# Longer waits between the bundles of the block inverse and ahead of the chain's first factors, in a hybrid decoder step on one core

## The chip, the cores and the metric

The kernel runs on 1 core of a Trainium2 chip. The metric is device time in microseconds of one launch, as the median of several runs; lower is better.

## What is computed

One step of a decoder layer: 2048 prompt tokens and 64 sample tokens (8 sequences of 8) go through two parallel head groups (sliding-window attention with sinks, and RWKV-7 with a matrix state), an output projection and a ConvFFN, each between RMS norms. Cut to what matters here:

```python
def step(S, inp):                        # RWKV-7, one token after the other
    r_t, w_t, k_t, v_t, kk_t, a_t = inp
    sa = einsum('bhij,bhj->bhi', S, kk_t)
    S = S * w_t - sa * (kk_t * a_t) + v_t * k_t
    return S, einsum('bhij,bhj->bhi', S, r_t)

proj = rms_norm(x) @ w_in                # q, k, v and the RWKV features
mix  = concat([attention(q, k, v), rwkv7(features)]) @ w_out
x    = x + rms_norm(mix)
x    = x + rms_norm(conv_ffn(rms_norm(x)))
```

All is in float32, and the outputs are both activations and the new caches and states.

## The kernel before

**Dense work.** The 2112 columns are cut into five groups of 448, 448, 448, 384 and 384. Each group has a projection `P[g]` (20 tasks of 24 matmuls), an output projection `O[g]` (8 tasks) and an FFN `F[2g]`, `F[2g+1]` (66 tasks). Every product is made of three matmuls of rounded halves (high by high, high by low, low by high), so that a task is 24 matmuls of 448 or 384 columns, named `gm` or `pf` in the trace; there are 470 tasks and 11,280 such matmuls. For each task ScalarE makes the high half of the weights (`wh`) and VectorE the low half (`wl`), two tasks ahead. A projection also spawns side streams (`pair`, `rest`, `norms`: matmuls `pw`, `pa`, `pd`, `pb`) that make the RWKV factors `ar` and `bk` and store them to memory as `abd`.

**Recurrent work.** The 32 chunks of 64 tokens are worked off in nine units of 3 or 4 chunks; a unit also holds one or two blocks of attention. `Mixer.unit` runs, for a unit, `scores` (matmuls `sc_e`, `sc_o` give each chunk's tile `G`), then `invert`, then `chain`, `groupnorm` and `finish`.

- `invert` (line 1011) inverts the triangular 32 by 32 blocks of `G`. It takes them through memory (`dgr`) into one tile `gb`, in which all blocks of a unit lie side by side, runs 31 steps of two VectorE instructions each (lines 1045 and 1046, on `tmp` and `tt`), in bundles of four, copies the result on ScalarE (line 1049), stores it twice (`dxr`, `dtr`), and loads it back into `G` (line 1059) and into the tiles `zt` (line 1088; two buffers). Then each chunk takes two groups of eight small matmuls (`pz`) with a ScalarE copy behind each.
- `chain` (line 1134) goes through the chunks in order, since each needs the state `S` that the one before left: transposes `vt` and `bkt` of the loaded values and factors (`ab<-abd`), matmuls `pc`, a ScalarE copy, `pu`, a ScalarE copy, `pS`, and two VectorE instructions that make the next `S` (lines 1175 and 1176).
- `groupnorm` and `finish` normalise on VectorE, transpose (`pt`), multiply by the gate (`pg`) and store to `od` (`od<-fin`), which `O[g]` loads (`r<-od`). `O[0]` needs units 0 and 1.

**The order.** The program is written as generators. `Flow` keeps a clock of its own, `Clock.t`, that adds up nominal matmul times in nanoseconds. A stream that yields a number N may go on once half of N has gone by on that clock (line 239 of `Flow.step`); between two dense matmul triples `Flow.tick` takes one step of a side stream and one of the unit in work. Where a stage needs something that isn't done, `Flow.force` runs the other streams with no dense work between them. A unit starts when the one before it has ended. The tile framework's scheduler then orders each engine's queue by this order and by its own view of what is ready. Each engine takes its queue strictly in order, and all transfers are issued by SyncE's queue.

`Flow.step` holds the line that turns a wait into planner's time:

```python
s.at = self.clock.t + (0.0 if callable(w) else 0.5 * (self.LAG if w is None else w))
```

The dense stages stand in this order:

```python
order = [P[0], P[1], P[2], O[0], P[3], F[0], O[1], F[1], P[4], F[2], O[2], ...]
```

Of the kernel before, what the change touches and what calls it, by code (L numbers as in the profile page):

```python
# [967 lines left out]
class Mixer:  # L968
# [43 lines left out]
    def invert(self, Gs):  # L1012

        nc, sp, v, te = self.nc, self.sp, self.nc.vector, self.te
        n = len(Gs)
        nb = n * 16
        dg = self.dp.tile([64, 1024], F32, tag="dg", name="dgr")

        def blocks(G, d, c):

            for b in range(2):
                for e in range(2):
                    q, r = slice(64 * e + 32 * b, 64 * e + 32 * b + 32), 16 * c + 8 * b + 4 * e
                    yield G[q, e::2, q], d[r:r + 4, :].rearrange("h (s t) -> s h t", t=32)

        for c, G in enumerate(Gs):
            for x, y in blocks(G, dg, c):
                nc.sync.dma_start(out=y, in_=x)
        yield 3000
        gb = self.b4([128, 32, 32], "gb", "ab")  # L1030
        nc.sync.dma_start(out=gb[:nb], in_=dg[:nb, :].rearrange("q (s t) -> q s t", t=32))
        tt = self.b4([128, 32, 32], "tt", "ab")

        tmp = sp.tile([128, 256], F32, tag="ivt", name="tmp", bufs=1)
        nc.gpsimd.memset(tt[:nb], 0.0)
        nc.gpsimd.memset(tt[:nb].rearrange("q s t -> q (s t)")[:, 0:1024:33], 1.0)
        yield 5000
        for j in range(31):
            if j and j % 4 == 0:
                yield 1500  # L1040
            m, w = 31 - j, j + 1
            col = gb[:nb, j, w:].unsqueeze(2).to_broadcast([nb, m, w])
            row = tt[:nb, j, 0:w].unsqueeze(1).to_broadcast([nb, m, w])
            tm = tmp[:nb, 0:m * w].rearrange("q (m w) -> q m w", w=w)
            v.tensor_tensor(out=tm, in0=col, in1=row, op=ALU.mult)  # L1045
            v.tensor_tensor(out=tt[:nb, w:, 0:w], in0=tt[:nb, w:, 0:w], in1=tm, op=ALU.subtract)  # L1046
        yield 1500
        xx = gb
        nc.scalar.copy(out=xx[:nb], in_=tt[:nb].rearrange("q s t -> q t s"))
        yield 1500  # L1050
        dx = self.dp.tile([64, 1024], F32, tag="dx", name="dxr")
        nc.sync.dma_start(out=dx[:nb, :], in_=xx[:nb].rearrange("q s t -> q (s t)"))
        dt = self.dp.tile([64, 1024], F32, tag="dt", name="dtr")
        nc.sync.dma_start(out=dt[:nb, :], in_=tt[:nb].rearrange("q s t -> q (s t)"))
        yield 3000
        zts = []
        for c, G in enumerate(Gs):
            for x, y in blocks(G, dx, c):
                nc.sync.dma_start(out=x, in_=y)
            if c < 2:  # L1060
                zts.append(self.zt(dt, c))
        yield 5000
        for c, G in enumerate(Gs):
            if c + 2 < n:
                zts.append(self.zt(dt, c + 2))
            zt = zts[c]

            q = [(slice(64 * e, 64 * e + 32), slice(64 * e + 32, 64 * e + 64)) for e in range(2)]
            hd = [slice(32 * p, 32 * p + 32) for p in range(4)]
            pz = self.ps("pz")  # L1070
            for h in range(NH):
                x, y = q[h % 2]
                te.matmul(pz[y, hd[h // 2]], G[x, h, y], zt[x, hd[h // 2]], start=True, stop=True)
            for x, y in q:
                nc.scalar.copy(out=zt[y], in_=pz[y, 0:128])
            yield 2500
            pz = self.ps("pz")
            for h in range(NH):
                x, y = q[h % 2]
                te.matmul(pz[x, hd[h // 2]], zt[y, hd[h // 2]], G[y, h, y], start=True, stop=True)  # L1080
            for e, (x, y) in enumerate(q):
                nc.scalar.activation(out=G[x, e::2, y], in_=pz[x, 0:128].rearrange("p (h t) -> p h t", t=32), func=AF.Copy, scale=-1.0)
            yield 1500
# [50 lines left out]
    def chain(self, c0, n, Gs, ys):  # L1134

        nc, v, te, sh = self.nc, self.nc.vector, self.te, self.sh
        uvs, nxt = {}, self.factors(c0)

        def values(c):
            t, w = CH * (c0 + c), CH * min(2, n - c)  # L1140
            V = self.t2("vl", tag="vl", bufs=1).rearrange("p (q t) -> p q t", t=128)
            nc.sync.dma_start(out=V[:, :, :w], in_=sh.v[:, :, t:t + w].rearrange("q p t -> p q t"))
            return V

        V = values(0)
        yield 5000
        for c in range(n):
            if c % 2 == 0:
                m = min(2, n - c)
                pv = self.ps("vt")  # L1150
                for p in range(4):
                    te.transpose(pv[:CH * m, 128 * p:128 * p + 128], V[:, p, :CH * m], sh.ident)
                for i in range(m):
                    uvs[c + i] = self.t2("uv", tag="uv", bufs=2)
                    self.values(uvs[c + i], pv[64 * i:64 * i + 64])
                yield 1500
            (ars, bks), uv, G = nxt, uvs[c], Gs[c]
            bkt = self.bk_tok(bks, "bkt")
            yield 1500
            if c + 1 < n:  # L1160
                nxt = self.factors(c0 + c + 1)
                if c % 2:
                    V = values(c + 1)
            S, Sn = sh.S[self.si], sh.S[1 - self.si]
            self.si = 1 - self.si
            pc = [self.ps("pc", "o") for _ in range(2)]
            for p in range(4):
                for e, a in enumerate(HH):
                    te.matmul(pc[e][:, 64 * p:64 * p + 64], ars[p][a], S[a, p, :], half=True, start=p == 0, stop=False)
            yield from self.solve(G, uv, pc)  # L1170
            pS = self.ps("pS")[:, 0:256]
            for p in range(4):
                for e, a in enumerate(HH):
                    te.matmul(pS[a, 64 * p:64 * p + 64], heads(bkt, e)[:, p], heads(uv, e)[:, p], half=True, start=True, stop=True)
            v.tensor_tensor(out=Sn, in0=pS.rearrange("q (p d) -> q p d", d=64), in1=S, op=ALU.add)
            v.tensor_tensor(out=Sn, in0=Sn, in1=sh.EC[:, c0 + c, :].unsqueeze(2).to_broadcast([128, 4, 64]), op=ALU.mult)
            yield 500
            if c % 2 == 0:
                ys.append(self.t2("y", tag="y", bufs=2))
            self.outputs(ys[-1][HH[c % 2]], G, uv, pc)  # L1180
            yield 2000
# [282 lines left out]
def heads(t, e):  # L1464

    return t.rearrange("s (p e d) -> s e p d", e=2, d=64)[:, e]
# [207 lines left out]
```

## Time and profile before

| | |
|---|---|
| runs | 2900.69, 2896.43, 2889.96 us; median 2896.43 |
| profiled execution | 2903.55 us, of which the span 2901.8 us |
| TensorE busy (matmuls, ends modelled) | 2769.6 us, 95% of the span |
| VectorE, ScalarE, GpSimd busy | 1961.2, 1411.5, 265.7 us |
| mean granted TensorE clock | 0.969 of full speed |
| DMA | 446.60 MB, 154 GB/s in the mean |

The page lists, for one execution, the busy time of each engine, the span in 40 slices, the chain of work that ended last, and the costliest groups of instructions. The views asked of the trace are: who waited for whom, the timeline of one engine in a window, and the busy time of each engine in a window with the granted clock. A matmul's duration in the timeline is longer than the distance to the next one, since matmuls are pipelined: the distance between two dense matmuls of 448 columns in the timeline is 0.20 us.

### The profile page before, as it was taken

The numbers are of one execution on the slowest core, as the hardware profiler recorded it, in microseconds if no ns is written. First come the engines' busy times: TensorE is split into PE (matmuls) and PEld (weight loads), VectorE is DVE, ScalarE is ACT, GpSimd is POOL, SyncE is SP. The second block draws the span as 40 slices with busy tenths as digits, with TensorE's granted clock in tenths as the row PEclk, the third lists the DMA queues.
The fourth block names the chain that finished last, engine by engine and source line by source line (L and its number), as shares of the span: only waits on it lengthen the run. The fifth ranks groups of instructions, "written<-read, shape, count | busy, mean of one in ns | idle before, by whom it ended". The sixth has DMA issues, their size and how long they took to land.

```text
span 2901.8 us, 46432 instructions
## 1 busy us (share of the span) xinstructions
PE 2769.6 (95%) x17003; PEld 2403.4 (83%) x17003; DVE 1961.2 (68%) x3892; ACT 1411.5 (49%) x2621; POOL 265.7 (9%) x521
## 2 busy tenths in 40 slices
PE   8997999899999999989899999999999999999997
PEld 6775776678778888868688888888899999999997
DVE  6884796759665775599566675796645765566556
ACT  6554555555545545445554455555333444344432
POOL 0010011001101010011000010001001001011110
PEclk9997999989989999989899999999999999999998
DMA  6674545656644343565644434674433654345433
GB/s 197 199 207 130 177 139 174 189 176 186 182 129 128 124 133 119 160 210 163 179 133 131 131 113 138 218 230 123 125 109 110 195 175 127 128 143 167 129 126 104
DMA packets 312740, 446.60 MB, mean 154 GB/s; under 512 B 120648, under 2 KB 241160, under 8 KB 312496
## 3 DMA queue, kind: packets, MB, share of 16 engines
q1 hardware_dynamic: 312080, 443.48, 50.2%
q8 instruction: 134, 2.20, 0.3%
q14 instruction: 94, 0.77, 0.1%
q10 hardware_dynamic: 432, 0.16, 0.0%
HBM read 362.19 MB, written 76.97 MB: 151 GB/s over the span
## 4 chain that ended last, share of the span: by engine, by line
PE 52%; DVE 4%; DMA 2%; ACT 1%; issue 1%; SPq 0%; DVEq 0%; ACTq 0%
PE gm L185 32%; PE pf L185 14%; PE pc L185 1%; DVE wl L355 1%; PE ms L185 1%; ACT wh L354 0%; DMA r<-x2d 0%; PE po L185 0%; DMA w<-in_w 0%; PE sc L185 0%; PE sc_e L185 0%; PE pz L185 0%; PE ppt L189 0%; PE spc L185 0%; DMA r<-xnd 0%
## 5 line engine op out<-in xcount | busy, mean ns | idle before, releaser
L185 PE MATMUL gm<-xhi,wh 128*128 128x448 f32 (+3 forms) x2880 | 1045.9, 366 | 32.4 <-ACT xhi L354 11.1
L185 PE MATMUL gm<-xlo,wh 128*128 128x448 f32 (+4 forms) x2880 | 1035.9, 360 | 9.7 <-DVE xlo L355 9.6
L185 PE MATMUL gm<-xhi,wl 128*128 128x448 f32 (+4 forms) x2880 | 1032.6, 359 | 0.0
L354 ACT CAST wh<-w 128x1024 fp32r<-128x1024 f32 (+1 forms) x470 | 490.3, 1044 | 758.8 <-PE gm L185 408.5
L355 DVE TENSOR_TENSOR wl<-w,wh 128x1024 fp32r<-128x1024 f32 (+1 forms) x470 | 570.2, 1214 | 406.5 <-ACT wh L354 393.5
L185 PEld LDWEIGHTS gm<-xhi,wh 128*128 128x128 f32 (+2 forms) x2880 | 542.5, 189 | 100.0 <-issue 24.3
L185 PEld LDWEIGHTS gm<-xlo,wh 128*128 128x128 f32 (+2 forms) x2880 | 543.8, 189 | 58.5 <-DVE xlo L355 16.7
L185 PEld LDWEIGHTS gm<-xhi,wl 128*128 128x128 f32 (+2 forms) x2880 | 543.3, 189 | 40.2 <-issue 8.6
L185 PE MATMUL pf<-hh,wh 128*128 128x448 f32 (+1 forms) x880 | 319.5, 363 | 4.4 <-DVE c L895 2.7
L185 PE MATMUL pf<-hl,wh 128*128 128x448 f32 (+1 forms) x880 | 316.3, 359 | 0.0
L185 PE MATMUL pf<-hh,wl 128*128 128x448 f32 (+1 forms) x880 | 316.0, 359 | 0.0
L885 POOL COPY zcar<-zz 128x2 f32<-128x2 f32 x110 | 87.7, 797 | 1443.4 <-ACT zz L874 1443.4
L912 DVE TENSOR_TENSOR acc<-acc,pf 128x448 f32<-128x448 f32 (+1 forms) x200 | 117.9, 592 | 102.3 <-PE pf L185 101.6
L185 PEld LDWEIGHTS pf<-hh,wh 128*128 128x128 f32 x880 | 167.3, 190 | 21.0 <-issue 6.1
L185 PEld LDWEIGHTS pf<-hl,wh 128*128 128x128 f32 x880 | 167.5, 190 | 11.0 <-issue 2.8
L185 PEld LDWEIGHTS pf<-hh,wl 128*128 128x128 f32 x880 | 167.1, 190 | 10.6 <-issue 2.0
L881 DVE SCALAR_TENSOR_TENSOR c<-zz,c_cw,c 128x448 f32<-128x448 f32 (+2 forms) x220 | 140.9, 640 | 16.1 <-ACT c L875 13.3
L895 DVE TENSOR_TENSOR c<-c,gm 128x448 f32<-128x448 f32 (+1 forms) x110 | 65.1, 592 | 88.2 <-PE gm L185 78.8
L888 ACT ACTIVATE c<-c 128x448 f32<-128x448 f32 (+1 forms) x110 | 61.4, 558 | 129.3 <-DVE c L881 95.9
L1045 DVE TENSOR_TENSOR tmp<-gb,tt 64x31 f32<-64x31 f32 (+37 forms) x310 | 102.4, 330 | 7.8 <-DMA gb<-dgr 3.5
L1046 DVE TENSOR_TENSOR tt<-tt,tmp 64x31 f32<-64x31 f32 (+37 forms) x310 | 102.7, 331 | 4.4
L680 POOL COPY carry<-h 128x1 f32<-128x1 f32 (+1 forms) x70 | 45.4, 649 | 622.5 <-ACT h L678 622.3
(271 smaller groups left out, 3190.9 us busy)
## 6 DMA issues: line engine op xcount, KB each, us to landing
w<-in_w SPq DMA_DIRECT2D x220, 512.0 KB
w<-in_w2q SPq DMA_DIRECT2D x100, 512.0 KB
w<-in_w_all SPq DMA_DIRECT2D x90, 512.0 KB
ab<-abd SPq DMA_DIRECT2D x66, 512.0 KB
w<-in_w_out SPq DMA_DIRECT2D x40, 512.0 KB
r<-in_xT SPq DMA_DIRECT2D x40, 224.0 KB
r<-in_xT SPq DMA_DIRECT2D x32, 192.0 KB
r<-od SPq DMA_DIRECT2D x24, 224.0 KB
```

The costliest lines, as they stand in the source:

```text
L185: return self.te.matmul(out, lhsT, rhs, **kw)
L354: self.nc.scalar.copy(out=hi, in_=src)
L355: self.nc.vector.tensor_tensor(out=lo, in0=src, in1=hi.bitcast(F32), op=ALU.subtract)
L680: nc.gpsimd.tensor_copy(out=s.next[:m, i, :].unsqueeze(2), in_=hs[:, :, s.nl:])
L881: v.scalar_tensor_tensor(out=c[:, :npr], in0=z[:, j:j + npr], scalar=cw(j), in1=c[:, :npr], op0=ALU.mult, op1=ALU.add)
L885: nc.gpsimd.tensor_copy(out=sh.zcar[:, f, :], in_=z[:, npr:npr + 2])
L888: nc.scalar.activation(out=c, in_=c, func=AF.Silu)
L895: v.tensor_tensor(out=c, in0=c, in1=ps, op=ALU.mult)
L912: v.tensor_tensor(out=accs[c], in0=accs[c], in1=ps, op=ALU.add)
L1045: v.tensor_tensor(out=tm, in0=col, in1=row, op=ALU.mult)
L1046: v.tensor_tensor(out=tt[:nb, w:, 0:w], in0=tt[:nb, w:, 0:w], in1=tm, op=ALU.subtract)
```

## The change

Six numbers that streams yield are larger; no instruction is added or removed.

```diff
@@ invert
         nc.gpsimd.memset(tt[:nb].rearrange("q s t -> q (s t)")[:, 0:1024:33], 1.0)
-        yield 5000
+        yield 9000
         for j in range(31):
             if j and j % 4 == 0:
-                yield 1500
+                yield 6000
...
                 zts.append(self.zt(dt, c))
-        yield 5000
+        yield 14000
         for c, G in enumerate(Gs):
...
                 nc.scalar.copy(out=zt[y], in_=pz[y, 0:128])
-            yield 2500
+            yield 4000
             pz = self.ps("pz")
@@ chain
         V = values(0)
-        yield 5000
+        yield 9000
         for c in range(n):
```

Half of each number is planner's time: the step between two bundles of the inverse goes from 0.75 to 3.0 us of `Clock.t`, the wait for `zt` from 2.5 to 7.0, the one between the two `pz` groups from 1.25 to 2.0, the first factors' from 2.5 to 4.5. Counted along TensorE's dense matmuls, the changed program differs in these places.

TensorE's queue at the end of `P[1]`, where unit 0's inverse comes back (`pz`) and its chain begins (`vt`, `bkt`, `pc`, `pu`). Before:

```order
L185 MATMUL gm<-xhi,wl 128x448
L185 MATMUL pz<-zt,G 32x32
L189 MATMUL ppt<-c_ident,s 128x128 x2
L185 MATMUL pz<-zt,G 32x32 x7
L189 MATMUL ppt<-c_ident,s 128x128 x2
L185 MATMUL pz<-G,zt 32x32 x8
L189 MATMUL ppt<-c_ident,s 128x128 x4
L185 MATMUL po<-pT,va 64x512
L185 MATMUL pz<-zt,G 32x32 x8
```

And with the change:

```order
L185 MATMUL gm<-xhi,wl 128x448
L185 MATMUL pz<-G,zt 32x32
L185 MATMUL pz<-zt,G 32x32
L185 MATMUL pz<-G,zt 32x32 x7
L185 MATMUL pb<-b_2779,c_blockones 128x448
L185 MATMUL pz<-zt,G 32x32 x7
L185 MATMUL pw<-ls,lw_149 128x448
L185 MATMUL pz<-G,zt 32x32 x8
L185 MATMUL pz<-zt,G 32x32 x8
L185 MATMUL pz<-G,zt 32x32 x8
L185 MATMUL pz<-zt,G 32x32 x8
L185 MATMUL pz<-G,zt 32x32 x8
```

The first `pz` stood behind dense matmul 864 and stands behind 954 now, of the 960 of `P[0]` and `P[1]`; the attention's `ppt` and `po` are no longer among them, and the run of matmuls without a dense one, 100 long at 864, is 126 long at 960. The last step of the inverse moves from 864 to 927, counted by the dense matmuls ahead of it in the program.

TensorE's queue where unit 1's inverse comes back. Before, this is in the last fifth of `P[2]`, whose last dense matmul is 1439:

```order
L185 MATMUL gm<-xhi,wh 128x448
L185 MATMUL pz<-zt,G 32x32 x7
L185 MATMUL gm<-xlo,wh 128x448
L185 MATMUL gm<-xhi,wl 128x448
L185 MATMUL po<-pT,va 64x512
L185 MATMUL pz<-G,zt 32x32 x8
L185 MATMUL pz<-zt,G 32x32 x8
L185 MATMUL pz<-G,zt 32x32 x8
```

With the change:

```order
L185 MATMUL gm<-xhi,wl 128x448
L185 MATMUL pa<-ls,lw_153 128x448
L185 MATMUL pd<-d_160,sel_159 128x448
L185 MATMUL pb<-b_4644,c_blockones 128x448
L185 MATMUL pz<-zt,G 32x32 x8
L185 MATMUL pz<-G,zt 32x32 x8
L185 MATMUL pz<-zt,G 32x32 x8
L185 MATMUL pz<-G,zt 32x32 x8
L185 MATMUL pz<-zt,G 32x32 x8
L185 MATMUL pz<-G,zt 32x32 x8
L189 MATMUL vt<-c_ident,vl 128x128 x4
L189 MATMUL bkt<-c_ident,ab 128x128 x4
```

The `gm` ahead of it is the last of `P[2]`. The `pz` of unit 1 moved from 1331 to 1344 to behind 1440, and with them the whole chain, `groupnorm` and `finish` of the unit; 167 small matmuls follow each other there. The last step of the inverse moves from 1300 to 1435. Behind them stand 36 dense matmuls of `O[0]` that read the attention's half of `od`, and then the first that read unit 1's.

TensorE's queue in `P[3]`, at the start of unit 2's chain. Before:

```order
L185 MATMUL pz<-zt,G 32x32 x8
L185 MATMUL pz<-G,zt 32x32 x8
L189 MATMUL vt<-c_ident,vl 128x128 x4
L185 MATMUL pc<-S_117,ab 128x64
L189 MATMUL bkt<-c_ident,ab 128x128 x4
L185 MATMUL pc<-S_117,ab 128x64 x7
L185 MATMUL pc<-uv,G 64x64 x8
L185 MATMUL pu<-rhs,G 64x64 x8
L185 MATMUL pS<-uv,bkt 64x64
```

With the change:

```order
L185 MATMUL pz<-zt,G 32x32 x8
L185 MATMUL pz<-G,zt 32x32 x8
L185 MATMUL pz<-zt,G 32x32 x8
L185 MATMUL pz<-G,zt 32x32 x8
L189 MATMUL vt<-c_ident,vl 128x128 x4
L185 MATMUL gm<-xhi,wh 96x384
L185 MATMUL gm<-xlo,wh 96x384
L185 MATMUL gm<-xhi,wl 96x384
L185 MATMUL gm<-xhi,wh 96x384
```

Before, 125 matmuls without a dense one follow each other here, behind dense matmul 1728; now the longest such run is 36, at 1752, and 23 dense ones stand between `vt` and `bkt`.

## Rows read from the trace of the kernel before

**Rows 1.** The page's busy times, and the view of the core's span and clock.

```profile
PE 2769.6 (95%) x17003; PEld 2403.4 (83%) x17003; DVE 1961.2 (68%) x3892; ACT 1411.5 (49%) x2621; POOL 265.7 (9%) x521
...
core 0: 2901.8 us, clock 0.969
```

**Rows 2.** Who TensorE waited for: us in total, times, longest us.

```profile
PE pz L185 <- DMA zt<-dtr: 12.3, 7, 8.2
...
PE pb L185 <- DVE b L745: 8.0, 5, 2.5
...
PE pz L185 <- ACT zt L1075: 4.1, 7, 0.9
...
PE bkt L189 <- DMA ab<-abd: 3.6, 1, 3.6
```

**Rows 3.** Windows: length, busy (count) of PE, PEld, DVE, ACT, POOL, clock, DMA.

```profile
197.00:241.00 44.00, 40.60 (x180) 33.10 (x180) 41.37 (x110) 23.32 (x61) 2.71 (x8) 0.96 0.44 134
241.00:320.00 79.00, 61.98 (x594) 45.67 (x592) 32.26 (x63) 37.59 (x84) 2.99 (x10) 0.81 0.59 157
249.00:281.00 32.00, 23.44 (x217) 14.46 (x217) 9.29 (x14) 13.55 (x35) 2.04 (x4) 0.57 0.58 156
380.00:427.00 47.00, 45.22 (x216) 37.93 (x215) 46.43 (x119) 22.10 (x45) 10.09 (x11) 1.00 0.48 143
427.00:501.00 74.00, 71.54 (x581) 53.09 (x580) 46.07 (x97) 40.66 (x83) 8.82 (x13) 0.93 0.53 155
571.00:620.00 49.00, 43.88 (x377) 33.51 (x377) 28.26 (x69) 24.87 (x55) 1.69 (x4) 0.81 0.52 144
```

**Rows 4.** Timeline, unit 0's inverse and chain start: start us, us, engine, line, [idle before <-releaser].

```profile
242.78 0.51 SPq L1052 DMA_DIRECT2D dxr<-gb  x1
...
240.81 1.94 ACT L1049 COPY gb<-tt 64x1024 f32<-64x1024 f32 x1 [5.35 <-DVE tt L1046]
...
249.42 0.28 PE L185 MATMUL pz<-zt,G 32*32 32x32 f32 x2 [8.21 <-DMA zt<-dtr]
...
262.19 1.11 PE L189 MATMUL vt<-c_ident,vl 128*128 128x128 f32 x4
265.17 1.86 PE L185 MATMUL pb<-b,c_blockones 128*128 128x448 f32 x2 [1.85 <-DVE b L745]
...
272.11 1.09 PE L189 MATMUL bkt<-c_ident,ab 128*128 128x128 f32 x4 [3.63 <-DMA ab<-abd]
```

**Rows 5.** TensorE's timeline, one chunk of unit 0's chain at full clock.

```profile
283.74 1.11 PE L185 MATMUL pc<-S,ab 64*128 64x64 f32 x16
284.78 0.68 PE L185 MATMUL pc<-uv,G 64*64 64x64 f32 x16
...
286.20 0.78 PE L185 MATMUL pu<-rhs,G 64*64 64x64 f32 x16
...
288.81 0.47 PE L185 MATMUL gm<-xhi,wh 128*128 128x448 f32 x1
289.12 0.36 PE L185 MATMUL gm<-xlo,wh 128*128 128x448 f32 x1
289.32 0.36 PE L185 MATMUL gm<-xhi,wl 128*128 128x448 f32 x1
```

**Rows 6.** Timelines of three engines, unit 1's groupnorm and finish, and the start of `O[0]`.

```profile
474.07 0.68 DVE L1188 TENSOR_REDUCE st<-y 64x8 f32<-64x512 f32 x1
...
486.71 0.68 DVE L1199 TENSOR_TENSOR y<-y,rsg 64x512 f32<-64x512 f32 x1
...
491.49 0.38 SPq L358 DMA_DIRECT2D od<-fin  x1
...
496.08 0.37 SPq L358 DMA_DIRECT2D od<-fin  x1
...
487.70 0.74 PE L189 MATMUL pt<-c_ident,y 64*128 64x64 f32 x3
...
504.44 0.47 PE L185 MATMUL gm<-xlo,wh 128*128 128x448 f32 x1 [2.78 <-DVE xlo L355]
```

## The prediction

> **What bounds the kernel now.** I first read the busy times: TensorE is busy 95% of the span, at a mean clock of 0.969 [rows 1]. So no term can be large: what can be won is TensorE's idle time and the time in which its clock is granted at half, that is, at 1.2 instead of 2.4 GHz. The table of waits then says whom TensorE stood idle for. The inverse and the first factors have 12.3 us behind the transfer of `zt`, 4.1 behind ScalarE's copy into it and 3.6 behind the load of `ab`; side streams have others, such as 8.0 at `pb` behind VectorE [rows 2]. That is 20 us by name. But an idle stretch also costs clock, so I read the windows next, and in each one the loss as idle time plus busy time times what the clock lacks of 1 [rows 3]. In the 79 us from 241 (unit 0's inverse comes back and its chain runs) TensorE idles 79.0 - 62.0 = 17.0 us, and 62.0 x 0.19 = 11.8 go with the clock: 29 us, the dearest stretch that the change touches. In 571 to 620 (unit 2's) it is 5.1 + 43.9 x 0.19 = 13.4, in 427 to 501 (unit 1's chain) 2.5 + 71.5 x 0.07 = 7.5.
>
> Why unit 0 comes back so late is in the same view: from 197 to 241, while its inverse is computed, VectorE is busy 41.4 of 44 us, and from 380 to 427 (unit 1's) 46.4 of 47 [rows 3]. VectorE, not the planner's 0.75 us, paces the inverse. Its last step ends just before ScalarE's copy at 240.81; TensorE has run into `pz` by then and waits until 249.42 [rows 4].
>
> **Part one: the wait for `zt` and `ab` at the end of `P[1]`.** In the program before, the first `pz` of unit 0 stood right behind the last step of the inverse (both at dense matmul 864). Now 27 dense matmuls lie between (927 and 954). One takes 0.20 us (289.12 to 289.32 [rows 5]), so they cover 5.4 of the 8.6 us from 240.81 to 249.42 [rows 4]; about 3 of the 8.2 remain, a gain of 5. The 3.6 at `bkt` and the 1.9 at `pb` [rows 4] go, since the factors are fetched 4.5 planner's us before they are used and the side streams' groups now stand apart in the queue: 5.5. The remaining idle of the window (17.0 - 8.2 - 3.6 - 1.9 = 3.3) stays, and so does half of the clock: from 249 to 281 TensorE was busy 23.4 us at 0.57 [rows 3], which lost 10.1, and the run of small matmuls there is 126 long now, no shorter than before; I take 5. With 3 more for the stretch up to 241 (3.4 idle and 40.6 x 0.04 of clock), where the inverse no longer crowds VectorE, this is **-19 us**. Bounds: -5, if only the `zt` wait shrinks, and -29, the whole loss of the window.
>
> **Part two: unit 2 in `P[3]`.** The run of 125 small matmuls becomes short runs with dense ones between; nothing new is waited for. Of the 13.4 us, half of the idle and three quarters of the clock's part go: 2.6 + 6.3, **-9 us** (0 to -13).
>
> **Part three: the other units.** There remain 12.3 - 8.2 = 4.1 us behind `zt` and 4.1 behind ScalarE's copy [rows 2], against planner's waits that grow from 2.5 to 7.0 and from 1.25 to 2.0 us. I take all 8 as gone: **-8 us** (0 to -15, the latter with as much in clock).
>
> **Part four: what is now late, `O[0]`.** Unit 1 starts when unit 0 has ended and now ends later itself; `O[0]` needs it. Before, the two just met: the last store to `od` is issued at 496.08, and the first dense matmuls of `O[0]` wait only 2.8 us, at 504.44 [rows 6]. Now all of `P[2]`'s dense matmuls stand ahead of the first `pz` of unit 1, and the last step of the inverse is only five of them earlier. From there to the first matmul on unit 1's rows, nothing of `P[2]` is left to cover:
>
> - inverse to first `pz`: 8.6 us, as for unit 0 [rows 4];
> - three chunks of `pz`: four took 12.8 (249.42 to 262.19 [rows 4]), with six matmul groups of the attention between; taken 6 (at most 9.6);
> - `vt` and the copies behind it: 3, twice the way from `pc` to `pu` (284.78 to 286.20 [rows 5]);
> - three chunks: 283.74 to 288.81 is 5.1 [rows 5], with the two VectorE instructions for the new state some 6 each: 18;
> - `groupnorm`: 13.3 us from 474.07 to 487.39 [rows 6], shared with other VectorE work; taken 7;
> - `finish`: 487.70 to 496.08, 8.4 us [rows 6];
> - store, load and split: 242.78 to 249.42 is 6.6 for a store and the loads behind it [rows 4]; taken 7.
>
> That is 58; the first half of the rows is stored 4.6 us earlier (491.49 against 496.08 [rows 6]), so 53. Of these, 36 dense matmuls of `O[0]` cover 7, and about 18 are TensorE's own work on this chain, which it had to do anyway (three times some 4.3, of which 1.11, 0.68 and 0.78 stand in [rows 5], and 5 for the rest). Idle: 53 - 1 - 7 - 18 = 27; at the clock of unit 0's bare run (0.57), the 18 cost 8 more: 35. What it replaces: the 7.5 of unit 1's chain in `P[2]`, the 2.8 at `O[0]`, and some 3 of the crowded window from 380, since VectorE's 31 steps are spread over a longer piece of `P[2]`. Net **+22 us**. Bounds: +5 (a chain at the pace of its own instructions, idle 12) and +40 (`pz` and `groupnorm` at their upper figures, all at half clock).
>
> **The sum.** -19 - 9 - 8 + 22 = -14 us on the profiled execution's 2903.55 (span 2901.8 and 1.75 around it), that is 2889. That run lies 7.1 above the median of the runs, 2896.43, for which I forecast **2882**.
>
> The Trainium skill ("TensorE: Matmul & The Clock Gate", section "What's actually happening") puts the cost of the clock's ramp at under 1% of a typical kernel's span and advises against fitting it. The trace does not agree: a mean clock of 0.969 is 3.1% of the span, 90 us [rows 1].
>
> **Rivals.**
>
> *No change.* VectorE paces the inverse, whatever the planner's clock says, and the chain between `P[2]` and `O[0]` runs no faster than it did at 241 to 320, where four chunks, from the inverse's end to the end of their chain, filled the window's 79 us. Without the 96 dense matmuls between (20 us) that is 59, for three chunks 44, against 36 in my first four rows: 8 more, and with 3 more at the clock the sum is -3: 2893. For it: VectorE's 94 to 99% [rows 3]. Against it: 79 us contain the waits at `ab` and `pb`.
>
> *Slower.* The price is set by the length of runs without a dense matmul. Before, there were three such runs of 100, 67 and 125, which lost 29, 7.5 and 13.4; now there are two, 126 and 167 long. If both cost what the dearest did, 0.29 us for each small matmul, it is 84 against 50: +34, with the -8 of the other units +26: 2922. It decides when each of the two runs ends in a transfer, as the run at 241 did, and the one before `O[0]` ends in three (`zt`, `ab`, `od`). Against it: 427 to 501 held 581 matmuls and lost little, because dense ones stood between.
>
> *The clock costs nothing.* If the half clock falls only where TensorE waits anyway, the clock's terms drop out: part one gives 14, part two 3, part three 8, and part four costs 27 - 2.5 - 2.8 - 3 = 19: -6, 2890. This is what the page's rule above comes to. The window 249 to 281, busy 23.4 us of 32 at 0.57 [rows 3], speaks against it.
>
> **How the numbers follow.** My forecast's case, a gain of 5 to 45 us, has 0.50; no change 0.24; slower 0.20; the clock for nothing 0.06. A measurement of this kernel can tell about 0.5% (14 us) from no change, so the forecast's own time stands at that border: within its case I give a gain over 0.5% four fifths, because part four is counted piece by piece with little overlap: 0.40, and 0.05 from the others. Slower by over 0.5%: four fifths of the slower rival and a little of the no-change case: 0.19. The range goes from 2849 (the first three parts at their lower bounds, part four at +10) to 2924 (the slower rival).
>
> **What would show it.** Right: no wait at `bkt` behind `ab`; the waits of `pz` for `zt` under 6 us in total outside the stretch before `O[0]`; a new idle time of 20 to 35 us on TensorE just before `O[0]`, in pieces behind `zt`, ScalarE, VectorE and `od`, at a clock well under 1; unit 2's stretch at a clock over 0.95; the same count of instructions. Wrong: `O[0]` starting as soon as `P[2]` ends, which would make part four a gain; VectorE as full as before while TensorE waits at `pz` as long as before; or new stalls in `P[4]`, where unit 6's inverse now falls among the projection's pairs, for which I have no term.

## The result, and the profile after

| | before | changed |
|---|---|---|
| runs beside each other | 2896.44 us (2886.02 to 2900.69, 8 runs) | 2909.64 us (2903.79 to 2918.09, 8 runs) |
| ratio, 95% interval | | 1.0052 [1.0034, 1.0070] |
| profiled execution | 2903.55, span 2901.8 | 2906.23, span 2904.5 |

The changed kernel is 13 us slower, where the prediction had it 14 us faster; the interval reaches to both sides of the 0.5% that it took as the border of "no change". The profiled executions lie 7 above the median of before and 3 below that of the changed kernel, so the two traces differ by 3 us only. For that reason a second trace of the kernel before is used below (label before_again, 2881.90 us). One correction to the text ahead: the diff enlarges five numbers, not six.

The page's busy times of the changed kernel, and its span and clock, against [rows 1]:

```profile
PE 2770.7 (95%) x17003; PEld 2401.8 (83%) x17003; DVE 1962.9 (68%) x3892; ACT 1410.6 (49%) x2623; POOL 267.3 (9%) x521
...
core 0: 2904.5 us, clock 0.969
```

The sums are the same to a thousandth, but for GpSimd's (0.6% more); ScalarE counts two more instructions, both loads of its function tables. Whom TensorE waited for in the changed kernel (us in total, times, longest), against [rows 2]:

```profile
PE gm L185 <- ACT h L678: 13.1, 5, 5.1
PE rb_ps L185 <- DVE nr L51: 8.0, 1, 8.0
PE pb L185 <- DVE b L745: 7.9, 3, 4.9
...
PE ms L185 <- DVE dg L787: 7.1, 3, 3.8
...
PE pz L185 <- ACT zt L1075: 3.2, 6, 0.7
...
PE pz L185 <- DMA zt<-dtr: 2.0, 5, 0.7
```

The waits that the change aimed at are gone: 2.0 us behind `zt` in place of 12.3, none at `bkt` behind `ab`. In their place stand waits of the projection's pairs and of the norms: 13.1 at `h`, 8.0 at `nr`, 7.1 at `dg` (at `b` it is 7.9, as before). Two of these in the kernel before:

```profile
PE ms L185 <- DVE dg L787: 5.2, 3, 3.1
...
PE gm L185 <- ACT h L678: 4.1, 2, 2.5
```

Where the time went is read best along the dense work, which is the same in both kernels. I cut the span at the first matmul of tasks 30, 50, 80, 140 and 300 (task 40 begins `P[2]`, 60 `O[0]`, 68 `P[3]`, 162 `P[4]`, 182 `F[2]`), and take `P[4]` by itself as the fifth line. Windows of the kernel before, with the columns of [rows 3]:

```profile
201.20:402.30 201.10, 176.84 (x1132) 133.09 (x1131) 141.85 (x326) 101.17 (x227) 13.68 (x38) 0.91 0.55 157
402.30:691.10 288.80, 266.46 (x1871) 208.82 (x1870) 211.10 (x497) 155.26 (x342) 25.33 (x42) 0.92 0.59 176
691.10:1100.70 409.60, 403.47 (x2608) 338.56 (x2607) 282.54 (x613) 210.00 (x397) 45.49 (x58) 0.97 0.47 141
1100.70:2131.50 1030.80, 992.55 (x6404) 846.63 (x6403) 712.70 (x1469) 513.21 (x961) 83.46 (x166) 0.98 0.50 154
1256.50:1380.70 124.20, 116.61 (x646) 98.20 (x646) 112.42 (x252) 69.16 (x155) 25.14 (x68) 0.99 0.63 188
```

The same five of the changed kernel:

```profile
199.80:363.00 163.20, 157.06 (x1075) 123.99 (x1074) 127.71 (x283) 95.15 (x215) 21.16 (x36) 0.95 0.60 177
363.00:662.50 299.50, 265.59 (x1851) 208.36 (x1849) 211.93 (x503) 155.81 (x340) 30.44 (x44) 0.90 0.58 171
662.50:1074.50 412.00, 402.20 (x2654) 333.67 (x2653) 286.21 (x606) 204.72 (x389) 30.09 (x58) 0.99 0.47 140
1074.50:2134.20 1059.70, 1014.92 (x6436) 860.38 (x6435) 724.44 (x1513) 523.43 (x984) 87.89 (x166) 0.97 0.50 152
1239.90:1394.40 154.50, 138.99 (x822) 110.89 (x822) 115.17 (x271) 76.32 (x174) 28.68 (x68) 0.93 0.55 162
```

And the second trace of the kernel before, in the first four stretches:

```profile
200.40:398.20 197.80, 175.74 (x1131) 131.88 (x1131) 141.77 (x326) 101.09 (x227) 16.20 (x38) 0.91 0.56 160
398.20:679.60 281.40, 260.19 (x1871) 204.54 (x1871) 211.02 (x497) 154.83 (x341) 25.85 (x42) 0.95 0.61 180
679.60:1080.30 400.70, 395.17 (x2608) 331.19 (x2607) 282.36 (x613) 209.39 (x397) 44.46 (x58) 1.00 0.48 145
1080.30:2111.90 1031.60, 993.66 (x6404) 848.23 (x6403) 712.88 (x1469) 513.29 (x962) 81.51 (x166) 0.98 0.50 154
```

The reader should take the first number behind each window. Against the mean of the two traces of before (201.1 and 197.8, 288.8 and 281.4, 409.6 and 400.7, 1030.8 and 1031.6), the changed kernel gains 36 us in tasks 30 to 49, loses 14 in 50 to 79, 7 in 80 to 139 and 28 in 140 to 299: together 13, which is the difference of the medians. (Small matmuls count where they stand: 57 fewer stand in tasks 30 to 49 of the changed kernel, so that some 5 us of its gain there, an estimate from the pace of their forms, are work moved over the cut.) Up to task 139 the change is a gain of 15; the loss is behind that, where the prediction had a small gain. The fifth line names the place: `P[4]` takes 154.5 us in place of 124.2. There 176 more matmuls stand in it, most of them unit 6's, so part of the length is work that stood elsewhere before; but TensorE also idles 15.5 us in place of 7.6, and the clock is granted at 0.93 in place of 0.99.

The local windows of the changed kernel, in the order unit 0's inverse, unit 0's `pz` and first chunk, unit 1's inverse, the stretch ahead of `O[0]`, unit 2's chain:

```profile
196.00:251.00 55.00, 55.00 (x256) 45.13 (x257) 51.94 (x127) 33.66 (x80) 13.01 (x16) 1.00 0.65 191
...
258.00:285.00 27.00, 22.36 (x280) 16.84 (x280) 9.51 (x16) 13.53 (x38) 0.31 (x2) 0.68 0.52 147
...
383.00:436.00 53.00, 48.87 (x226) 38.49 (x227) 50.31 (x127) 25.40 (x52) 17.67 (x15) 1.00 0.57 163
436.00:500.00 64.00, 47.78 (x449) 36.82 (x448) 29.18 (x71) 27.13 (x62) 0.20 (x1) 0.73 0.58 165
...
575.00:650.00 75.00, 65.67 (x636) 52.69 (x635) 45.02 (x82) 42.12 (x95) 6.81 (x16) 0.86 0.63 198
```

In the first, VectorE is as full as before (51.9 of 55 us) and TensorE does not wait at all, at full clock. In the fourth, 16.2 us are idle and 47.8 x 0.27 = 12.9 go with the clock: 29 where the chain of unit 1 lost 7.5 before. TensorE's timeline of that stretch:

```profile
445.46 1.83 PE L185 MATMUL pb<-b,c_blockones 128*128 128x448 f32 x2 [4.88 <-DVE b L745]
...
453.11 1.11 PE L189 MATMUL vt<-c_ident,vl 128*128 128x128 f32 x4
...
486.70 1.07 PE L189 MATMUL pt<-c_ident,y 64*128 64x64 f32 x3 [2.64 <-DVE y L1199]
488.77 1.47 PE L189 MATMUL pt<-c_ident,y 128*128 128x128 f32 x4 [1.01 <-ACT fin L1219]
...
499.46 1.49 PE L185 MATMUL gm<-xhi,wh 128*128 128x448 f32 x3
```

The first matmul on unit 1's rows comes at 499.46, 63 us after unit 1's inverse ended, at the window's start: the bare chain that the prediction described, 10 us longer than its 53, with the scores of the next unit queued in its last part.

### The profile page after: what moved, and what is told of

The parts are those of the page before. It is cut to its first block, busy times and chain, and to the rows that moved or that the text cites. A ratio compares the mean times of both kernels' runs of the same rounds, so it can differ in the third digit from the quotient of the medians.

```text
span 2904.5 us, 46415 instructions
## 1 busy us (share of the span) xinstructions
PE 2770.7 (95%) x17003; PEld 2401.8 (83%) x17003; DVE 1962.9 (68%) x3892; ACT 1410.6 (49%) x2623; POOL 267.3 (9%) x521
## 4 chain that ended last, share of the span: by engine, by line
PE 48%; DVE 2%; DMA 2%; ACT 1%; issue 1%; SPq 0%; DVEq 0%; ACTq 0%
PE gm L185 30%; PE pf L185 13%; PE pc L185 1%; DVE wl L355 1%; PE ms L185 1%; DMA r<-x2d 1%; DMA r<-od 0%; DMA r<-xnd 0%; ACT wh L354 0%; PE spc L185 0%; DVE acc L945 0%; PE pz L185 0%; PE sc_e L185 0%; PE pu L185 0%; DVE sa L773 0%
## 5 line engine op out<-in xcount | busy, mean ns | idle before, releaser
L185 PE MATMUL gm<-xhi,wh 128*128 128x448 f32 (+3 forms) x2880 | 1054.6, 368 | 47.6 <-ACT h L678 13.1
L185 PE MATMUL gm<-xlo,wh 128*128 128x448 f32 (+3 forms) x2880 | 1039.0, 361 | 1.8 <-DVE xlo L355 1.6
L185 PE MATMUL gm<-xhi,wl 128*128 128x448 f32 (+3 forms) x2880 | 1034.3, 360 | 0.0
L355 DVE TENSOR_TENSOR wl<-w,wh 128x1024 fp32r<-128x1024 f32 (+1 forms) x470 | 570.4, 1214 | 419.0 <-ACT wh L354 413.9
L885 POOL COPY zcar<-zz 128x2 f32<-128x2 f32 x110 | 81.6, 742 | 1479.0 <-ACT zz L874 1479.0
L1045 DVE TENSOR_TENSOR tmp<-gb,tt 64x31 f32<-64x31 f32 (+37 forms) x310 | 102.8, 332 | 6.5 <-DMA gb<-dgr 2.1
L1046 DVE TENSOR_TENSOR tt<-tt,tmp 64x31 f32<-64x31 f32 (+37 forms) x310 | 103.1, 333 | 4.5
L354 ACT CAST xhi<-r 128x448 fp32r<-128x448 f32 (+1 forms) x112 | 59.0, 543 | 86.4 <-DVE r L549 32.4
```

What stands on the lines that cost most here:

```text
L185: return self.te.matmul(out, lhsT, rhs, **kw)
L354: self.nc.scalar.copy(out=hi, in_=src)
L355: self.nc.vector.tensor_tensor(out=lo, in0=src, in1=hi.bitcast(F32), op=ALU.subtract)
L885: nc.gpsimd.tensor_copy(out=sh.zcar[:, f, :], in_=z[:, npr:npr + 2])
```

## The experiments

All variants come from one of the two kernels. "The loss of a stretch", in the expectations, is its length less what its matmuls take where nothing holds them (for each form of matmul, the mean of the smaller half of the distances to the next one at full clock); it counts waits, half clock and the gaps between small matmuls together. Each ratio is to the kernel before run beside the variant, whose median was 2890 to 2894 us; the first expectations reckon from 2896. The units are switched one by one with a tuple in `invert` and `chain`, in which 9 stands for the sample tokens:

```diff
-        yield 5000
+        yield 9000 if u in LONG else 5000
...
-                yield 1500
+                yield 6000 if u in LONG else 1500
```

and so at the other three places.

**Which unit.** Unit 0 alone (long_u0):

```diff
+        LONG = (0,)
```

> The five longer waits for unit 0 alone, the old ones for units 1 to 9. The changed kernel's trace shows some 29 us less loss while unit 0's inverse comes back (tasks 30 to 49), 11 more around the start of O[0], and some 20 to 30 more in later stretches. Theory A (each unit's waits act on that unit's own stretch, and what is late behind it): unit 0's gain stays, unit 1 still meets O[0] late (its pz stand at dense matmul 1440, as in the changed kernel), and the later losses go: 2896 - 29 + 11 = 2878 (2868 to 2888). Theory B (the gain is given back wherever TensorE gets ahead, since VectorE's work has to be done anyway): within 5 us of the kernel before, 2891 to 2901.

Measured: 2912.34 us, ratio 1.0089 [1.0065, 1.0112]. All units but 0 and 1 (long_u2to9):

```diff
+        LONG = (2, 3, 4, 5, 6, 7, 8, 9)
```

> The old waits for units 0 and 1, the longer ones for units 2 to 9. Theory A (each unit's waits act on its own stretch): units 2 to 9 carry the whole loss of the changed kernel and the gain of unit 0 is gone, so 2896 + 20 to 30 = 2916 to 2926. Theory B (the gain of unit 0 is given back by a VectorE that is behind): without the gain nothing is given back, 2891 to 2901. The prediction on record, parts two and three: a gain of 8 to 17, 2879 to 2888.

Measured: 2883.80, ratio 0.9986 [0.9969, 1.0003]. Theory A missed both, in opposite directions. Theory B missed the first, and its second range is met by the ratio only (0.9986 of 2896 is 2892): the unit that gained is the one that makes the kernel slow, and units 2 to 9, which I had taken for the place of the loss, are harmless when units 0 and 1 are left alone. (Their time is within what parts two and three of the prediction give, but its interval reaches no change.) In the trace of the first, tasks 30 to 49 take 163.7 us, as in the changed kernel, but tasks 50 to 79 take 324.0, and `P[4]` 151.6. In the second, `P[4]` takes 121.9. So the long waits of unit 6 are not what makes `P[4]` dear; something that starts with unit 0 is.

**Which wait.** The inverse's two numbers alone (inv_only), and the three behind the inverse alone (back_only):

```diff
-        yield 5000
+        yield 9000
...
-                yield 1500
+                yield 6000
```

> The longer waits inside the inverse only (9000 ahead of it, 6000 between bundles), for all units; the waits for zt, between the pz groups and for the first factors as before. If the bundles' wait is what moves units, it has unit 0's gain in part (the last step stands at dense matmul 926, pz at 960) and the late O[0] (pz of unit 1 at 1445): 2900 to 2915, like the changed kernel. If the waits behind the transfers are what brings the gain, the wait for zt of some 8 us stays at each pz and it is slower than the changed kernel: 2915 to 2930.

```diff
-        yield 5000
+        yield 14000
...
-            yield 2500
+            yield 4000
...
-        yield 5000
+        yield 9000
```

> The longer waits behind the inverse only (14000 for zt, 4000 between the pz groups, 9000 for the first factors), for all units; the inverse's bundles as before. Unit 0's inverse and pz stay at dense matmul 864 in one run, so its loss of some 49 us in tasks 30 to 49 stays within 10, and unit 1's chain stays in P[2]. If the bundles' wait is what matters: 2888 to 2900. If the waits behind the transfers are (the prediction's part three, 8 to 15 us): 2878 to 2888.

Measured: 2888.41, ratio 0.9998 [0.9978, 1.0017], and 2898.79, ratio 1.0036 [1.0019, 1.0053]. The first is below both of its ranges, the second within that of the bundles' wait. The first has tasks 30 to 49 in 176.8 us: nearly two thirds of unit 0's gain come from the bundles' wait. The second has them in 199.6: no gain at all. So the waits behind the transfers, from which the prediction's part three expected its gain, gain nothing by themselves. In both, unit 6's inverse stands some 95 dense matmuls ahead of its old place (4145 to 4320 and 4149 to 4342; it is 163 in the changed kernel); `P[4]` takes 152 us, but most of that is moved work, since tasks 140 to 299 take 1034.6 and 1037.0.

**The stretch ahead of `O[0]`.** A second look at the kernel before (before_again):

> The kernel before once more, for a second trace of it: its runs lie between 2877 and 2903, and the trace shown is of one at 2903.6. If the difference between its runs is spread over the whole program, each ten tasks lose a little less than in the first trace; if it comes from one or two stretches (theory: those where side streams and a unit's recurrence meet, tasks 60 to 79 and 160 to 189), it stands there, with 5 to 15 us each.

Measured: 2881.90 us. Tasks 70 to 79 lose 10 us less than in the first trace and 90 to 99 lose 8 less; every other ten tasks agree within some 3, those of `P[4]` included. Of the theory's two places the first came out, tasks 160 to 189 did not.

`O[0]` freed of unit 1, in the changed kernel (after_O0_free) and in the one before (before_O0_free):

```diff
+        if g == 0:
+            need = need - {("R", 1)}
...
-        self.source(S, lambda k: sh.o[k, :, t0:t0 + n])
+        self.source(S, (lambda k: a["xT"][:, k, t0:t0 + n]) if g == 0 else (lambda k: sh.o[k, :, t0:t0 + n]))
```

> The changed kernel, except that O[0] does not wait for unit 1 and multiplies the rows of x in place of those of od (the result of the first 448 columns is left out). Unit 1's chain then runs among the matmuls of O[0] and P[3]. Theory A (the late unit 1 in front of O[0] eats unit 0's gain): tasks 60 to 79 lose some 65 to 75 us in place of 103, and the run is 25 to 40 us shorter than the changed kernel: 2865 to 2882. Theory B (TensorE cannot keep its lead since VectorE is behind anyway): the loss moves to the next stretches, within 10 of the changed kernel: 2895 to 2907.

> The same edit to the kernel before: O[0] does not wait for unit 1 and multiplies rows of x (the result of the first 448 columns is left out). It shows what the edit itself saves where unit 1 is in time: the wait of 2.8 us at the start of O[0] and some clock. Theory A: 2880 to 2890, that is 0 to 10 less than the kernel before. Theory B: the same.

Measured: 2873.27, ratio 0.9929 [0.9902, 0.9956], and 2900.18, ratio 1.0026 [1.0010, 1.0043]. With `O[0]` free the change is a gain of 27 us. But the trace says that this is not only the stretch ahead of `O[0]`: against the changed kernel, tasks 50 to 79 take 256.0 in place of 299.5, tasks 80 to 139 take 432.1 in place of 412.0 (unit 1's chain moved there), and tasks 140 to 299 take 1037.2 in place of 1059.7, with `P[4]` at 126.3. Nothing was edited at task 140 and later. What did move there are the units: unit 6's inverse stands at dense matmuls 4248 to 4391 in this program, at 4079 to 4248 in the changed one, and at 4242 to 4378 in the kernel before. (The freed kernel before is some 10 us above what both theories allowed, and a quarter of a per cent slower than the kernel before. In its trace tasks 140 to 299 take 1038.8 us, and 7 of the 8 more stand in tasks 260 to 279, 130.4 against 123; why is open.)

The longer waits for all units but 0 (long_not0):

```diff
+        LONG = (1, 2, 3, 4, 5, 6, 7, 8, 9)
```

> The longer waits for units 1 to 9, the old ones for unit 0. Unit 1 starts where it did in the kernel before; its pz stand at dense matmuls 1322 to 1344, its chain's last pS at 1416, and only its groupnorm's end (pt) falls behind the last matmul of P[2], at 1440. Theory A (what costs is how much of unit 1 is left behind P[2]'s last matmul): only the 8 to 15 us of groupnorm and finish stand bare there, so it is 8 to 15 slower than the run with old waits for units 0 and 1 (2884): 2892 to 2899. Theory B (unit 1's own longer waits cost nothing, only unit 0's do): 2880 to 2888.

Measured: 2903.09, ratio 1.0038 [1.0023, 1.0053]. Slower by more than theory A allowed. In its trace the two middle stretches together (50 to 139) take 688.8 us, against 676.6 where units 0 and 1 have the old waits, and `P[4]` 139.4 against 121.9; unit 6's inverse stands at 4173 to 4344. That made a third theory.

**Theory C: the planner's own clock.** Where a stage needs something that isn't done and no stream is due, `Flow.force` sets `Clock.t` forward. In the planner's log of the two programs these jumps sum to 26 us before and to 53 in the changed kernel; ahead of `O[0]`, where unit 1's long waits now run without dense work, it is 29 in place of 2. A unit starts when the one before it has ended and `Clock.t`, less what units have used, has reached its due time. Units 1 to 5 are 28 us or more behind their due times in both programs, so the jump does not bring them forward (units 3 to 5 start 108 to 312 dense matmuls later in the changed kernel, behind longer units). Unit 6 waits for its due time in the changed kernel and nearly so before: it starts at dense matmul 3885 in place of 4029, and its inverse falls from the end of `P[4]` (matmuls 3888 to 4367) into its middle. In `P[4]` VectorE is busy 112.4 of 124.2 us (the window of before above). The planner's starts of units 6 to 8 can be shifted (after_u6_later, from the changed kernel):

```diff
+        starts = starts[:6] + [x + 27e3 for x in starts[6:]]
```

> The changed kernel with the planner's starts of units 6 to 8 27 us later, so that unit 6's inverse stands at dense matmuls 4245 to 4392 (end of P[4]) and not at 4079 to 4248 (its middle); units 0 to 5 stand as in the changed kernel. Theory C (the planner's forced wait ahead of O[0] moves its clock on and so starts the later units some 27 us of dense work early, where unit 6's inverse meets the pairs of P[4] and unit 8's end the start of F[4]): tasks 160 to 189 lose some 74 us in place of 94, tasks 260 to 279 some 22 in place of 28, and the run is 20 to 30 us shorter than the changed kernel: 2880 to 2890. Theory A alone (the cost lies only in front of O[0]): no change from the changed kernel, 2904 to 2912.

Measured: 2881.42, ratio 0.9964 [0.9950, 0.9979]. With -27e3 in long_u2to9 (u2to9_u6_early):

> The kernel with old waits for units 0 and 1 and the longer ones for units 2 to 9 (2884 us), with the planner's starts of units 6 to 8 27 us earlier: unit 6's inverse moves from dense matmuls 4245 to 4392 into the middle of P[4], 4077 to 4249, as in the changed kernel, while the stretch ahead of O[0] is that of the kernel before. Theory C: tasks 160 to 189 lose some 94 us in place of 74, 15 to 25 us longer: 2899 to 2909. Theory A alone: 2880 to 2888.

Measured: 2902.13, ratio 1.0027 [1.0009, 1.0045]. With -27e3 in the kernel before (before_u6_early):

> The kernel before with the planner's starts of units 6 to 8 27 us earlier: unit 6's inverse, with the old waits, moves from dense matmuls 4242 to 4378 to 4086 to 4255, into the middle of P[4]. Theory C, if the place of unit 6 is what counts: 5 to 20 us slower than before, 2895 to 2910, with the loss in tasks 160 to 189 (86 before). If only the longer waits make the place matter: 2885 to 2895.

Measured: 2910.36, ratio 1.0056 [1.0035, 1.0077]. With +27e3 in long_u2to9 (u2to9_u6_late):

> The kernel with old waits for units 0 and 1 and the longer ones for units 2 to 9 (2884 us), with the planner's starts of units 6 to 8 27 us later: unit 6's inverse leaves P[4] (matmuls 4365 to 4556; P[4] ends at 4368). Theory C: tasks 160 to 189 lose less than 74 us, 60 to 70: 2865 to 2880, faster than both kernels. If the end of P[4] is as good as the FFN behind it: 2880 to 2888.

Measured: 2871.94, ratio 0.9925 [0.9903, 0.9948]: faster than both kernels. All four came out as theory C said, but for small misses: `before_u6_early` lies 0.4 us above its range, and `u2to9_u6_late` loses 56 us in tasks 160 to 189 where 60 to 70 were expected.

| kernel | unit 6's inverse | `P[4]`, us | tasks 160 to 189, loss | tasks 140 to 299, us |
|---|---|---|---|---|
| before (two traces) | 4242 to 4378 | 124.2, 125.5 | 87, 86 | 1030.8, 1031.6 |
| changed | 4079 to 4248 | 154.5 | 94 | 1059.7 |
| before_u6_early | 4086 to 4255 | 162.3 | 97 | 1045.1 |
| u2to9_u6_early | 4077 to 4249 | 153.2 | 95 | 1049.9 |
| long_u2to9 | 4245 to 4392 | 121.9 | 74 | 1032.8 |
| after_u6_later | 4245 to 4392 | 122.2 | 76 | 1034.3 |
| u2to9_u6_late | 4365 to 4556 | 119.5 | 56 | 1016.8 |

In the last column the rows go by the place of the inverse, not by its waits, and in `before_u6_early` nothing but the starts of units 6 to 8 was edited. The price of the early place is 14 to 25 us in tasks 140 to 299, of which 10 to 21 stand in tasks 160 to 189, where unit 6 is; by the ratios of the runs it is 12 to 25 us. Tasks 140 to 299 of `before_u6_early` and of `after_u6_later`:

```profile
1088.10:2133.20 1045.10, 1008.06 (x6348) 857.84 (x6347) 710.48 (x1469) 513.17 (x955) 83.67 (x166) 0.97 0.49 152
...
1072.20:2106.50 1034.30, 1002.94 (x6439) 850.10 (x6439) 729.04 (x1519) 523.99 (x985) 79.37 (x166) 0.98 0.50 156
```

The place does not settle all. Where the inverse stands between the two groups, the stretch takes 1034.6 (inv_only), 1037.0 (back_only), 1037.9 (long_not0) and 1044.0 (long_u0, at 4149 to 4320, the place of inv_only within a few matmuls). Units 7 and 8 were shifted with unit 6 and are not told apart from it.

**What moves the starts, and what the waits are worth.** If the jump is the cause, taking it out of the planner's account must cure the changed kernel without an edit to the starts (after_jump_out; it takes out every jump, those of the kernel before too, so that unit 6's inverse comes later than there, at 4362 to 4533):

```diff
                 self.clock.t = max(now, min(wait))
+                self.mixed += self.clock.t - now
```

> The changed kernel, except that the time by which the planner's clock jumps where nothing dense can be placed is not counted toward the starts of units. Unit 6's inverse then stands at dense matmuls 4362 to 4533, behind P[4], while unit 1 is as late for O[0] as in the changed kernel. Theory C (the jump ahead of O[0] is what moves the later units into P[4]): tasks 160 to 189 lose 55 to 75 us in place of 94, tasks 260 to 279 some 22: 2868 to 2885. If something else in the changed kernel makes P[4] dear: 2900 to 2912.

Measured: 2873.25, ratio 0.9931 [0.9913, 0.9949]. Its windows of tasks 140 to 299 and of `P[4]`:

```profile
1072.50:2099.70 1027.20, 1001.75 (x6447) 849.93 (x6447) 733.83 (x1532) 519.30 (x983) 90.78 (x166) 0.99 0.51 157
1226.50:1343.40 116.90, 113.42 (x629) 97.80 (x630) 100.90 (x210) 62.92 (x136) 27.68 (x70) 0.98 0.65 194
```

`P[4]` takes 116.9 us in place of 154.5, with 3.5 idle in place of 15.5, though tasks 50 to 79 are as slow as in the changed kernel (305.8 against 299.5). Tasks 140 to 299 take 32 us less, and 80 to 139 (398.1 us) 14 less. So the 36 us between these two kernels were lost through the jumps' effect on the starts, and not in the stretch where the jump is. Putting back units 6 to 8 alone (after_u6_later) had returned 25 to 28 of them; the rest comes with places later than the old ones, and of the 14 in tasks 80 to 139 up to 9 may be the spread between traces of one kernel. The last two runs put unit 6 behind `P[4]` with the long waits of all units (after_u6_54), and with the old ones (before_u6_late, +27e3):

```diff
+        starts = starts[:6] + [x + 54e3 for x in starts[6:]]
```

> The changed kernel with units 6 to 8 started 54 us later, so that unit 6's inverse stands at 4365 to 4556 as in the fastest run so far (old waits for units 0 and 1, 2872). Theory C: all that is left between the two is unit 0's gain against unit 1's late end in front of O[0], in the trace -33 and +30 us up to task 99: within 6 us of that run, 2866 to 2878. If the late end costs more than the trace shows (long_not0 was 19 slower than the run without it): 2885 to 2895.

> The kernel before with units 6 to 8 started 27 us later and the old waits: unit 6's inverse at 4380 to 4489, behind P[4]. If the place of unit 6 alone makes the gain: 2866 to 2878, as with the longer waits. If the longer waits of units 2 to 9 gain by themselves (the prediction's parts two and three, 8 to 17 us): 2880 to 2890.

Measured: 2878.76, ratio 0.9945 [0.9925, 0.9964], and 2894.02, ratio 0.9998 [0.9979, 1.0017]. The first is 0.8 us above theory C's range, the second above both of its ranges. The place alone, with the old waits, gives nothing: `P[4]` falls to 118.3 us, but tasks 140 to 299 stay at 1030.8, so what `P[4]` gains is lost behind it. Long waits and a late unit 6 together give 15 to 22 us, but not in one stretch: `u2to9_u6_late` gains in tasks 140 to 299 (1016.8), while `after_u6_54`, with the same place and waits of unit 6, takes 1030.3 there and gains in tasks 30 to 49 (163.4). It is not told apart from `after_u6_later` either (0.9945 and 0.9964, intervals overlapping). Between the three kernels that have long waits and a late unit 6 (0.9925, 0.9931, 0.9945) the intervals overlap: whether units 0 and 1 take part is not told apart.

Who holds TensorE in `P[4]` of the changed kernel (waits in that window):

```profile
PE gm L185 <- ACT h L678: 5.4, 3, 2.3
PE pw L185 <- DVE e L753: 4.0, 1, 4.0
PE gm L185 <- ACT qraw L628: 2.6, 1, 2.6
```

And in after_jump_out:

```profile
PE ss_ps L185 <- ACT k L585: 3.0, 4, 1.1
PE gm L185 <- ACT xhi L355: 1.3, 1, 1.3
```

VectorE's timeline of the changed kernel at the wait for `e`:

```profile
1344.70 0.31 DVE L1046 TENSOR_TENSOR tt<-tt,tmp 64x156 f32<-64x156 f32 x1
1344.93 0.28 DVE L681 SCALAR_TENSOR_TENSOR v<-h,c_vec,hm 128x64 f32<-128x64 f32 x1
1345.13 0.29 DVE L1045 TENSOR_TENSOR tmp<-gb,tt 64x135 f32<-64x135 f32 x1
1345.34 1.22 DVE L355 TENSOR_TENSOR wl<-w,wh 128x1024 fp32r<-128x1024 f32 x1
1346.47 0.29 DVE L1046 TENSOR_TENSOR tt<-tt,tmp 64x135 f32<-64x135 f32 x1
1346.68 0.54 DVE L753 TENSOR_TENSOR e<-v,pb 128x384 f32<-128x384 f32 x1
```

And TensorE's:

```profile
1347.28 0.69 PE L185 MATMUL pw<-ls,lw 96*128 96x384 f32 x1 [4.00 <-DVE e L753]
...
1353.33 0.69 PE L185 MATMUL gm<-xhi,wh 128*128 128x384 f32 x1 [2.60 <-ACT qraw L628]
1353.81 0.52 PE L185 MATMUL gm<-xlo,wh 128*128 128x384 f32 x1
1354.13 0.52 PE L185 MATMUL gm<-xhi,wl 128*128 128x384 f32 x1
...
1358.18 0.33 PE L185 MATMUL gm<-xhi,wh 128*128 128x384 f32 x1
1358.35 0.33 PE L185 MATMUL gm<-xlo,wh 128*128 128x384 f32 x1
```

Nothing in VectorE's queue is long here. The inverse's steps (L1045, L1046) and the low halves of the weights (L355) stand between the pair's own instructions one by one. The pair is a chain over VectorE, TensorE and ScalarE, and each of its steps on VectorE comes a little later; TensorE meets the end of that chain at `pw` and again at `qraw`, and behind these waits the dense matmuls are 0.32 us apart (1353.81 to 1354.13), where they are 0.17 apart 4 us later. That is the reading of one place; no run took the inverse out of `P[4]` and left all else, so how the loss there divides among waits, clock and gaps is argued and not shown.

## Why the prediction was wrong

Its time, 2882, was 28 us under the median. The range, 2849 to 2924, held it, by luck: its upper end is that of the rival *Slower*, whose reason did not come out. By its own steps, from the cut stretches above:

- **Part one** (-19): the mechanism was right and the term too small. Tasks 30 to 49 are 36 us shorter, 5 of these by moved work. No wait is left at `bkt`, `pz` waits 2.0 us in all, and the inverse's 31 steps run beside a TensorE that is never idle (55.00 of 55.00 us at 1.00; before, 3.4 us of 44 idle at 0.96 [rows 3]). TensorE's idle time in the stretch fell from 24.3 and 22.1 us to 6.1, some 17, where the term held some 12; the clock's loss fell from 16 to 8, where it held some 6. The 6 that are left are not split further.
- **Part two** (-9): did not come in the changed kernel. Unit 2's window, 575 to 650, loses 9.3 us idle and 65.7 x 0.14 = 9.2 by the clock, against 13.4 before in a shorter window. The run of 125 small matmuls is broken up, as read from the order, but two waits took its place:

```profile
PE gm L185 <- ACT h L678: 7.6, 2, 5.1
PE ms L185 <- DVE dg L787: 3.8, 1, 3.8
```

Where units 0 and 1 kept the old waits, a gain did come: tasks 50 to 139 take 677, 679 and 682 us in `long_u2to9` and its two shifted variants, and 698, 682, 688 and 692 in the two traces of before and in the two variants of it that only shift units 6 to 8. In the mean that is 11 us less, with 16 us between the longest and the shortest of the four.

- **Part four** (+22): right in its total. The stretch ahead of `O[0]` lost 29 us where 35 were expected: less idle time (16 in place of 27) and more half clock (13 in place of 8). The 8 was worked out wrongly, since 18 us of work at full clock take 31.6 at 0.57, 14 more. Of the 13 that this was to replace, the 7.5 and the 2.8 went; the 3 of the window from 380 did not, idle time there is 4.1 us (383 to 436) in place of 1.8. That is +21. Parts two and four together were +13, and tasks 50 to 79 are 14 longer.
- **Part three** (-8) is the step that failed. It counted the waits of units 3 to 9 as if these units stood where they stood before, and only their waits shrank. They shrank (2.0 and 3.2 us are left behind `zt`), but tasks 80 to 299 are 35 us longer. Unit 6 had moved, by the planner's clock, which the change runs forward by 27 us more. With units 6 to 8 put back (after_u6_later) tasks 140 to 299 take 1034.3 us in place of 1059.7, and the kernel is 0.36%, 10 us, faster than the one before. Tasks 80 to 299 are then still 7 us longer and not 8 shorter, so part three's own gain was not seen; that this run comes near the forecast is due to the larger part one. The prediction had the fact in hand, since its last part says that unit 6's inverse now falls among the pairs of `P[4]` and that it has no term for it: a price put at nothing. A listing by unit, before against after, would have shown that unit 6 starts 144 dense matmuls earlier, and the 46.4 of 47 us that VectorE was busy beside the inverse [rows 3] was a sign of what such a meeting costs.
- **The rivals.** *No change* (VectorE paces) was wrong on unit 0. *Slower* was right in sign and wrong in place: it put +34 at the runs without a dense matmul in units 0 and 1. The two stretches with such runs are together 22 us shorter. *The clock costs nothing* is not borne out: the stretch ahead of `O[0]` ran at 0.73 and lost 12.9 us by it. The Trainium skill ("TensorE: Matmul & The Clock Gate", section "What's actually happening") puts the cost of the clock's ramp at under 1% of a typical kernel's span. The trace of the changed kernel does not agree either: its mean clock is 0.969 too, 3.1% of the span.

The sum, against the -14 of the forecast: 17 more gained in part one, 1 off in parts two and four, 43 off in part three, makes 27. Of the 43, 25 to 28 are unit 6's place by after_u6_later; the 15 that stay are the gain that was not seen and 7 us whose cause is open.

## What to carry to other kernels

Where a schedule is planned against a clock of its own, a longer wait at one place can move whatever waits for its due time by that clock: list where each later stage stands before and after, and price the new neighbours, before counting the waits that were aimed at. A gain at one place can be lost 1000 us later by work that nobody edited. The longer waits are worth having here (15 to 22 us), but only where the forced time does not start a later unit early: left out of the account (after_jump_out), or answered by later starts (after_u6_54, u2to9_u6_late).

## What was not expected of the hardware

The kernel before, run again and again, takes 2877 to 2905 us, a spread of 1%. Its two traces, 22 us apart, issue the same instructions in the same order, and differ in two stretches: tasks 50 to 79 (288.8 and 281.4 us, granted clock 0.92 and 0.95) and 80 to 139 (409.6 and 400.7 us, clock 0.97 and 1.00). In the second, TensorE idles 6.1 and 5.5 us, so that 8 of the 9 us are in its busy time. What decides between the two I did not find out. So a difference of up to 9 us in one stretch between single traces of two kernels shows little by itself; the main readings above rest on larger ones and on the medians of the runs.
